# S5 preparation in fewer, wider VectorE operations, and twelve of the first block's 24 gate tiles emitted from inside it

## The chip, the cores and the metric

One core of one Trainium2 chip runs the whole kernel. The metric is the device time of one execution in microseconds. Everything is fp32; matrix products against large weights are done as three fp32r products of split operands.

## The reference, cut to what matters

One layer of a streaming encoder is applied to 2048 + 16 prompt tokens and 64 sample tokens (2128 tokens of 1024 channels): a layer norm, one input projection, three recurrent branches (RWKV-7, S5, mLSTM), a gated sum of the branches, an output projection and a last layer norm.

```python
proj = (x @ p['w_in']).astype(F32)
rw_cols, rw_gate, s5_u, s5_gate, ml_qk, ml_v, ml_if, ml_o, ml_z, merge = split_cols(proj, IN_SIZES)
y_rw, ... = rwkv7_branch(rw_cols, rw_gate, ...)
y_s5, ... = s5_branch(s5_u, s5_gate, ...)
y_ml, ... = mlstm_branch(ml_qk, ml_v, ...)
gates = jax.nn.sigmoid(merge + p['b_merge']).reshape(x.shape[:2] + (N_BRANCH, D_MODEL))
merged = gates[..., 0, :] * (y_rw @ w_br_rw) + gates[..., 1, :] * (y_s5 @ w_br_s5) + gates[..., 2, :] * (y_ml @ w_br_ml)
# S5: lam_bar = exp(lam * dt); b_bar = ((lam_bar - 1) / lam) * b_mat
# hs = scan of lam_bar * h + b_bar @ u; y = real(c_mat @ hs) + d * u
```

The change touches two pieces: how the constant matrices of S5 are worked out on the chip (complex powers of `lam_bar`, times `b_bar` and `c_mat`), and when the `merge` columns of the projection are computed (24 tiles of 128 columns, the gate tiles).

## The kernel before, in words

The tokens are cut into five blocks; block 0 has 400 tokens, the next three 448, the last 384. In each block three generators run mixed by weights (`mix`): `rw_block` (six head pairs, each with a long chain of small operations), `ml_block`, and `s5_stream`. Each asks for projections: `proj` loads a 128-column tile of `w_in` and runs 24 matmuls on it (line 434, into PSUM tile `d`). In block 0 the tile comes raw from DRAM (line 404, two halves of 256 KB), ScalarE casts each half to `whi` (line 405), GpSimd subtracts to get `wlo` (line 406), and both go back to DRAM (line 411); later blocks load the split halves directly (line 425). Block 0 has 63 projections and 24 gate tiles, the same for the later blocks.

A gate tile is the same thing with its own buffers (`ghi`, `glo`, two halves each, so one tile deep; PSUM tile `f`, one buffer), then a tanh (line 1509) and a store. `gate_pass(b)` emits the 24 tiles after all generators of the block have ended. The activations `xh`, `xl` have one buffer each, so that the next block's copies land only when the last matmul of this block, a gate tile's, has read them. The raw weight buffers (three of them) are handed out in the order of emission, which is why no gate tile can start before the block's projections have been loaded.

`s5_setup` runs once, in block 0, as part of `s5_stream`: scalar work on 128x16 tiles, a table of powers per four state groups (`tab`, lines 1199 to 1212), the powers `pw`, the transposed C matrices, and a loop over 16 values of `q` (line 1259) that builds, per q, a scaled B (`bb`), `BL` (128x2x128), `CL` (128x2x144), two transposes (line 1274) and four K matmuls (line 1281). Its complex products go through `cmul`, six VectorE operations for each. All VectorE work of it is recorded at the helper's line 1132.

A scheduler orders each engine's instructions from the order of emission and from its own costs, so a change in emission reorders rows that the diff does not show. Loads, weight stores and the small transfers of the RWKV chain all stand in one queue, on SyncE.

Of the kernel before, what the change touches and what calls it, by code (L numbers as in the profile page):

```python
# [13 lines left out]
ALU = mybir.AluOpType  # L14
# [69 lines left out]
def tile_trunk(ctx: ExitStack, tc: tile.TileContext, I, O, dbg=None, parts=("rw", "s5", "ml", "mg")):  # L84
    nc = tc.nc
    V, S, G, PE = nc.vector, nc.scalar, nc.gpsimd, nc.tensor
    QQ = nc.sync
    blocks = make_blocks()
# [25 lines left out]
    def psum(shape, tag):  # L114
        return pt(ps, shape, tag, bufs=PSB[tag])
# [28 lines left out]
    TS = 8 * (NCM + 1)  # L144
# [970 lines left out]
    s5wo_d = pt(dram, (16, 128, 4, 128), "s5wo")  # L1115
# [6 lines left out]

    def s5_setup():
        A = [sA() for _ in range(4)]
        B = [sB() for _ in range(3)]
        nsm = [0]

        def sm():
            nsm[0] += 16
            return cut(A[1], nsm[0] - 16, (128, 16))  # L1130
# [46 lines left out]
        TT(pw[:, 0, 1], cs, zr, ALU.mult)  # L1177
        TT(pw[:, 1, 1], sn, zr, ALU.mult)

        def cmul(orr, oi, xr, xi, yr, yi, t):  # L1180
            TT(t, xi, yi, ALU.mult)
            TT(orr, xr, yr, ALU.mult)
            TT(orr, orr, t, ALU.subtract)
            TT(t, xi, yr, ALU.mult)
            TT(oi, xr, yi, ALU.mult)
            TT(oi, oi, t, ALU.add)

        for _ in range(3):
            double()
# [9 lines left out]
        for i in range(4):  # L1199
            tab = cut(flat("tab", TS), 0, (128, 4, 2, NCM + 1))  # L1200
            V.memset(tab[:, :, 0, 0:1], 1.0)
            V.memset(tab[:, :, 1, 0:1], 0.0)
            V.tensor_copy(tab[:, :, 0, 1], cs[:, 4 * i:4 * i + 4])
            V.tensor_copy(tab[:, :, 1, 1], sn[:, 4 * i:4 * i + 4])
            m = 1
            while m < NCM:
                n = min(m, NCM - m)
                o = slice(m + 1, m + 1 + n)
                y = [tab[:, :, ri, m:m + 1].to_broadcast((128, 4, n)) for ri in range(2)]
                cmul(tab[:, :, 0, o], tab[:, :, 1, o], tab[:, :, 0, 1:n + 1], tab[:, :, 1, 1:n + 1], y[0], y[1],  # L1210
                     cut(A[0], 288, (128, 4, 32))[:, :, :n])
                m *= 2
            nc.scalar.dma_start(s5t_d[i], tab.rearrange("p q r n -> p (q r n)"))
        yield
        ta = cut(A[0], 288, (128, 8, 16))
        for m in (1, 2, 4):
            b1 = lambda x: x[:, m:m + 1].to_broadcast((128, m, 16))
            cmul(pw[:, 0, m + 1:2 * m + 1], pw[:, 1, m + 1:2 * m + 1], pw[:, 0, 1:m + 1], pw[:, 1, 1:m + 1],
                 b1(pw[:, 0]), b1(pw[:, 1]), ta[:, :m])
# [3 lines left out]
        fr, fi, den, lm = sm(), sm(), sm(), sm()  # L1223
        TT(den, ar, ar, ALU.mult)
        TT(lm, ai, ai, ALU.mult)
        TT(den, den, lm, ALU.add)
# [24 lines left out]
        kz = cut(flat("tab", TS), 0, (16, 15, 16))  # L1251
        G.memset(kz[:, 0:7, :], 0.0)
        bt = cut(A[1], 336, (128, 2, 16))
        bb = cut(A[1], 304, (128, 2, 16))
        tb = cut(B[0], 256, (128, 9, 16))
        BL = cut(B[1], 0, (128, 2, 8, 16))
        CL = cut(B[2], 0, (128, 2, 9, 16))
        for q in range(16):
            for ri, nm in enumerate(("s5_b_re", "s5_b_im")):
                nc.sync.dma_start(bt[:, ri], I[nm][0, 2 * q:2 * q + 2].rearrange("a p h -> (a p) h"))  # L1260
            e = lambda x: x[:, q:q + 1].to_broadcast((128, 16))
            cmul(bb[:, 0], bb[:, 1], bt[:, 0], bt[:, 1], e(fr), e(fi), tb[:, 0])
            pe = lambda ri, n: pw[:, ri, 0:n, q:q + 1].to_broadcast((128, n, 16))
            pr = lambda ri: pwr[:, ri, :, q:q + 1].to_broadcast((128, 8, 16))
            be = lambda ri: bb[:, ri:ri + 1, :].to_broadcast((128, 8, 16))
            ce = lambda ri: cT[ri][:, q:q + 1, :].to_broadcast((128, 9, 16))
# [3 lines left out]
            wB = cut(w5(), 0, (128, 2, 128))  # L1270
            for ri in range(2):
                nc.scalar.dma_start(s5wo_d[q, :, 2 + ri, :], CL[:, ri, 1:9, :].rearrange("p j h -> p (j h)"))
                p = psum((128, 128), "o")
                PE.transpose(p, BL[:, ri].rearrange("p s h -> p (s h)"), ident)
                S.copy(wB[:, ri], p)
            nc.sync.dma_start(s5wi_d[q // 2, :, 2 * (q % 2):2 * (q % 2) + 2, :], wB)
            for g in range(2):
                r = slice(64 * g, 64 * g + 64)
                p = psum((16, 128), "o")
                for ri in range(2):  # L1280
                    PE.matmul(p, bb[r, ri, :], CL[r, ri, 0:8, :].rearrange("p j h -> p (j h)"),
                              start=ri == 0, stop=ri == 1)
                S.copy(kz[:, 7:15, :].rearrange("x j h -> x (j h)"), p)
                nc.scalar.dma_start(K_d[2 * q + g], kz)
            if q % 2:
                yield
        for g in range(2):
# [145 lines left out]
    def s5_stream(b):  # L1433
        for g in spend:
            yield from g
        d = yield from s5_proj(b)
        if b.first:
            yield from s5_setup()
            spend[:] = [s5_block(b, *d)]
        else:  # L1440
            spend[:] = []
            yield from s5_block(b, *d)

    def drain(g):
        for _ in g:
            pass
# [64 lines left out]

    def merge_pass():
        TBS = (768, 768, 576)
# [258 lines left out]
```

## Time and profile before

| | us |
|---|---|
| median of 3 runs (lowest to highest) | 4073.04 (4065.59 to 4080.69) |
| the profiled execution, its time | 4056.56 |
| its span, first to last instruction | 4054.6 |
| TensorE busy, share of the span | 3753.2, 93% |
| VectorE busy, share of the span | 2508.7, 62% |
| mean granted TensorE clock | 0.965 |

The windows below are cut where a new RWKV head pair starts (its first matmul at line 532): 186, 308, 424, 544 and 654 us in block 0, and 865 and 965 us for the first two head pairs of block 1. In `f` and `d` of the rows, `f` is a gate tile's PSUM tile and `d` a projection's.

### The profile page before, as it was taken

What the parts mean: (1) busy time and instruction counts of PE and PEld (TensorE: products, weight loads), DVE (VectorE), ACT (ScalarE), POOL (GpSimd) and SP (SyncE); (2) the same over time, 40 slices, a digit from 0 to 9 for tenths busy, and PEclk for the clock granted to TensorE, in tenths of its full rate; (3) what the DMA queues carried; (4) which work ended last, traced back from release to release, by engine and by line L of the source; (5) the groups of instructions that cost most, each with busy time, mean ns of one, the idle gap of its engine ahead of it and who ended that gap; (6) DMA issues with size and microseconds to landing.
All of it is one profiled execution on the core that took longest, in us unless ns stands there. A gap on an engine that the chain in (4) does not pass through costs nothing. (4 is left out here: it accounts for less than half of the span.)

```text
span 4054.6 us, 76802 instructions
## 1 busy us (share of the span) xinstructions
PE 3753.2 (93%) x27032; PEld 3319.8 (82%) x27032; DVE 2508.7 (62%) x8247; ACT 1204.0 (30%) x2626; POOL 669.3 (17%) x947
## 2 busy tenths in 40 slices
PE   6987778989999999999999999999999998999997
PEld 5876567878888878888878888878988887999997
DVE  7668885546556656656674665664675555457476
ACT  5433232323222222222232232223232232222222
POOL 5433132300000000000000000100000000233335
PEclk9988798999999999999999999999999998999999
DMA  8986378876657686666666565767677666566565
GB/s 255 290 250 198 89 223 238 273 246 189 202 185 225 193 254 188 194 195 203 204 214 219 170 212 183 219 203 225 219 228 229 202 200 172 159 195 206 153 188 161
DMA packets 820735, 836.67 MB, mean 206 GB/s; under 512 B 226118, under 2 KB 580654, under 8 KB 820350
## 3 DMA queue, kind: packets, MB, share of 16 engines
q1 hardware_dynamic: 737790, 759.00, 60.6%
q10 hardware_dynamic: 82560, 72.76, 6.0%
q8 instruction: 214, 3.51, 0.4%
q14 instruction: 171, 1.40, 0.1%
HBM read 635.40 MB, written 198.18 MB: 206 GB/s over the span
## 5 line engine op out<-in xcount | busy, mean ns | idle before, releaser
L434 PE MATMUL d<-xh,whi 128*128 128x448 f32 (+2 forms) x2520 | 940.3, 373 | 33.2 <-ACT whi L405 6.9
L434 PE MATMUL d<-xh,wlo 128*128 128x448 f32 (+2 forms) x2520 | 926.1, 368 | 5.8 <-POOL wlo L406 4.1
L434 PE MATMUL d<-xl,whi 128*128 128x448 f32 (+2 forms) x2520 | 924.6, 367 | 0.0
L434 PEld LDWEIGHTS d<-xh,whi 128*128 128x128 f32 x2520 | 481.5, 191 | 83.4 <-issue 17.4
L434 PEld LDWEIGHTS d<-xh,wlo 128*128 128x128 f32 x2520 | 480.9, 191 | 44.9 <-POOL wlo L406 8.1
L434 PEld LDWEIGHTS d<-xl,whi 128*128 128x128 f32 x2520 | 481.6, 191 | 34.0 <-issue 8.2
L406 POOL TENSOR_TENSOR wlo<-wraw,whi 128x512 fp32r<-128x512 f32 (+1 forms) x310 | 404.1, 1312 | 605.3 <-ACT whi L405 538.9
L434 PE MATMUL f<-xh,ghi 128*128 128x448 f32 (+2 forms) x912 | 348.1, 382 | 39.9 <-DMA ghi<-wsp 29.4
L434 PE MATMUL f<-xh,glo 128*128 128x448 f32 (+2 forms) x912 | 342.0, 375 | 3.0 <-DMA glo<-wsp 2.6
L434 PE MATMUL f<-xl,ghi 128*128 128x448 f32 (+2 forms) x912 | 337.9, 371 | 0.0
L405 ACT CAST whi<-wraw 128x512 fp32r<-128x512 f32 (+1 forms) x310 | 179.8, 586 | 421.5 <-PE z L1565 79.2
L618 DVE TENSOR_TENSOR Ztmp<-Uin,Z 128x60 f32<-128x60 f32 (+24 forms) x930 | 205.1, 221 | 117.8 <-DMA Uin<-Ud 105.2
L434 PEld LDWEIGHTS f<-xh,ghi 128*128 128x128 f32 x912 | 177.9, 195 | 60.5 <-DMA ghi<-wsp 21.7
L620 DVE TENSOR_TENSOR Z<-Z,Ztmp 128x60 f32<-128x60 f32 (+24 forms) x930 | 210.0, 226 | 13.0
L1565 PE MATMUL z<-ya,whi 128*128 128x384 f32 (+1 forms) x832 | 196.5, 321 | 0.0
L434 PEld LDWEIGHTS f<-xh,glo 128*128 128x128 f32 x912 | 177.4, 194 | 20.7 <-DMA glo<-wsp 6.4
L434 PEld LDWEIGHTS f<-xl,ghi 128*128 128x128 f32 x912 | 178.2, 195 | 10.5 <-issue 1.3
L946 DVE SCALAR_TENSOR_TENSOR X<-X,PT 128x448 f32<-128x448 f32 (+2 forms) x180 | 127.1, 706 | 42.9 <-ACT X L944 39.6
L1565 PEld LDWEIGHTS z<-ya,whi 128*128 128x128 f32 x832 | 144.4, 188 | 0.0
L1565 PE MATMUL z<-ya,wlo 128*128 128x384 f32 (+1 forms) x416 | 133.8, 322 | 0.0
L1565 PE MATMUL z<-yb,whi 128*128 128x384 f32 (+1 forms) x512 | 120.1, 320 | 2.1 <-DVE lq2i L251 1.8
L701 DVE COPY XV<-tr 64x512 f32<-64x512 f32 (+2 forms) x60 | 36.5, 614 | 134.9 <-ACT XV L700 134.2
(738 smaller groups left out, 6815.8 us busy)
## 6 DMA issues: line engine op xcount, KB each, us to landing
whi<-wsp SPq DMA_DIRECT2D x504, 256.0 KB
wlo<-wsp SPq DMA_DIRECT2D x504, 256.0 KB
ghi<-wsp SPq DMA_DIRECT2D x192, 256.0 KB
glo<-wsp SPq DMA_DIRECT2D x192, 256.0 KB
wraw<-in_w_in_dram SPq DMA_DIRECT2D x174, 256.0 KB
wsp<-whi SPq DMA_DIRECT2D x126, 256.0 KB
wsp<-wlo SPq DMA_DIRECT2D x126, 256.0 KB
w<-s5wo SPq DMA_DIRECT2D x80, 256.0 KB
```

The lines of the kernel that those rows point to most:

```text
L405: S.copy(h[:, :n, :M], raw[:, :n, :M])
L406: G.tensor_tensor(l[:, :n, :M], raw[:, :n, :M], h.bitcast(F32)[:, :n, :M], ALU.subtract)
L434: PE.matmul(p, a[k], c, start=i == 0, stop=i == 3 * KD - 1)
L618: V.tensor_tensor(t3, Uin[:, j:j + 1, j + 1:32].to_broadcast((128, m, n)), Z[:, 0:m, j:j + 1].to_broadcast((128, m, n)), ALU.mult)
L620: V.tensor_tensor(Z[:, 0:m, j + 1:32], Z[:, 0:m, j + 1:32], t3, ALU.add)
L701: V.tensor_copy(PX[hs[1], c0:c0 + n, 0:3:2, :], p[hs[1], :n])
L946: V.scalar_tensor_tensor(acc[:, :w], raw[:, j:j + w], pcol("conv_w", 12 * j + ti), acc[:, :w], ALU.mult, ALU.add)
L1565: PE.matmul(p, a[k], c[:, sl], start=i == 0, stop=i == n - 1)
```

## The change

Three things. First, `cmul` works on real and imaginary part together: two products of double width and two sums instead of four products and two sums, so four operations for six; the sign of `CL`'s imaginary part is folded into its last one, and `bb` is made for eight q at once (two loads of 8 q each, per part, where there were 32 small ones). Second, the two K products of a q share one PSUM tile and the two transposes share another; the K rows have two SBUF buffers; a q has one store of `CL` instead of two. Third, the gate tiles of block 0 become a generator, `gate1`, and `s5_stream` takes one tile from it each time `s5_setup` yields. It yields twelve times: eleven tiles stand between its steps and the twelfth behind its last; `gate_pass` drains the other twelve.

```diff
-        B = [sB() for _ in range(3)]
+        B = [sB() for _ in range(4)]
...
-        def cmul(orr, oi, xr, xi, yr, yi, t):
-            TT(t, xi, yi, ALU.mult)
-            TT(orr, xr, yr, ALU.mult)
-            TT(orr, orr, t, ALU.subtract)
-            TT(t, xi, yr, ALU.mult)
-            TT(oi, xr, yi, ALU.mult)
-            TT(oi, oi, t, ALU.add)
+        def cmul(out, x, yr, yi, u):
+
+            TT(out(None), x, yr, ALU.mult)
+            TT(u(None), x, yi, ALU.mult)
+            TT(out(0), out(0), u(1), ALU.subtract)
+            TT(out(1), out(1), u(0), ALU.add)
...
         for q in range(16):
-            for ri, nm in enumerate(("s5_b_re", "s5_b_im")):
-                nc.sync.dma_start(bt[:, ri], I[nm][0, 2 * q:2 * q + 2].rearrange("a p h -> (a p) h"))
-            e = lambda x: x[:, q:q + 1].to_broadcast((128, 16))
-            cmul(bb[:, 0], bb[:, 1], bt[:, 0], bt[:, 1], e(fr), e(fi), tb[:, 0])
...
-            cmul(BL[:, 0], BL[:, 1], be(0), be(1), pr(0), pr(1), tb[:, 0:8])
-            cmul(CL[:, 0], CL[:, 1], ce(0), ce(1), pe(0, 9), pe(1, 9), tb)
-            V.tensor_scalar(CL[:, 1], CL[:, 1], -1.0, None, ALU.mult)
+            if q % 8 == 0:
+                for ri, nm in enumerate(("s5_b_re", "s5_b_im")):
+                    nc.sync.dma_start(bb[:, ri], I[nm][0, 2 * q:2 * q + 16].rearrange("(q a) p h -> (a p) q h", a=2))
+                e = lambda x: x[:, None, q:q + 8, None].to_broadcast((128, 2, 8, 16))
+                TT(u8, bb, e(fi), ALU.mult)
+                TT(bb, bb, e(fr), ALU.mult)
+                TT(bb[:, 0], bb[:, 0], u8[:, 1], ALU.subtract)
+                TT(bb[:, 1], bb[:, 1], u8[:, 0], ALU.add)
...
+            cmul(at(BL, 1), pr, be(0), be(1), at(u8, 1))
...
+            TT(CL, pe, ce(0), ALU.mult)
+            TT(u9, pe, ce(1), ALU.mult)
+            TT(CL[:, 0], CL[:, 0], u9[:, 1], ALU.subtract)
+            V.scalar_tensor_tensor(CL[:, 1], CL[:, 1], -1.0, u9[:, 0], ALU.mult, ALU.subtract)
...
         if b.first:
-            yield from s5_setup()
+            for _ in s5_setup():
+                next(gate1)
+                yield
...
-    def gate_pass(b):
+    def gates(b):
         T = b.T
         for j in range(24):
...
             nc.sync.dma_start(g_d[b.i][128 * j:128 * j + 128, :], t[:, :T])
+            yield
+
+    gate1 = gates(blocks[0])
+
+    def gate_pass(b):
+        drain(gate1 if b.first else gates(b))
```

On VectorE, one q of the loop before (`sA` and `sB` are the scratch tiles that hold `bb`, `pw`, `BL`, `CL`):

```order
L1132 TENSOR_TENSOR sB_3107<-sA_3104 128x16
L1132 TENSOR_TENSOR sB_3108<-sA_3104,sB_3107 128x128 x2
L1132 TENSOR_TENSOR sA_3104<-sA_3104,sB_3107 128x16
L1132 TENSOR_TENSOR sB_3107<-sA_3104,sB_3107 128x128
L1132 TENSOR_TENSOR sB_3108<-sB_3108,sB_3107 128x128
...
L1132 TENSOR_TENSOR sB_3107<-sA_3106,sA_3103 128x144
L1132 TENSOR_TENSOR sB_3109<-sB_3109,sB_3107 128x144
...
L1269 TENSOR_SCALAR sB_3109<-sB_3109 128x144
```

And one q of the loop now:

```order
L1132 TENSOR_TENSOR sA_3104<-sB_3107,sB_3110 128x256
L254 TENSOR_TENSOR mqa_4698<-mrs_4696 128x2
L1132 TENSOR_TENSOR sB_3108<-sB_3108,sA_3104 128x128 x2
L255 SCALAR_TENSOR_TENSOR mqa_4698<-mqa_4698,mve_4694 128x2
L1132 TENSOR_TENSOR sA_3104<-sA_3103,sA_3106 128x288
...
L1132 TENSOR_TENSOR sB_3109<-sA_3103,sA_3105 128x288
L717 TENSOR_TENSOR Hw_4858<-tr_4859,Wc_3540 128x448
L1132 TENSOR_TENSOR sB_3109<-sB_3109,sA_3104 128x144
L1283 SCALAR_TENSOR_TENSOR sB_3109<-sB_3109,sA_3104 128x144
```

A q had 19 operations and has 8, with four more for every eight q; the elements that they pass over are nearly the same.

On GpSimd, the stretch that follows the third head pair's copy of `Wc` (line 554), before:

```order
L406 TENSOR_TENSOR wlo_5291<-wraw_5292,whi_5290 128x512
L406 TENSOR_TENSOR wlo_5485<-wraw_5486,whi_5484 128x512
L406 TENSOR_TENSOR wlo_5493<-wraw_5494,whi_5492 128x512
L198 TENSOR_TENSOR X_3673<-X_3673 128x2x64 x4
L449 MEMSET rv_5115 128x48
L406 TENSOR_TENSOR wlo_5866<-wraw_5867,whi_5865 128x512
```

And now:

```order
L406 TENSOR_TENSOR glo_4608<-wraw_4609,ghi_4607 128x512
L406 TENSOR_TENSOR glo_4616<-wraw_4617,ghi_4615 128x512
L406 TENSOR_TENSOR wlo_5049<-wraw_5050,whi_5048 128x512
L406 TENSOR_TENSOR glo_5004<-wraw_5005,ghi_5003 128x512
L406 TENSOR_TENSOR glo_5012<-wraw_5013,ghi_5011 128x512
L406 TENSOR_TENSOR wlo_5057<-wraw_5058,whi_5056 128x512
L406 TENSOR_TENSOR wlo_5186<-wraw_5187,whi_5185 128x512
```

Subtracts of gate tiles (`glo`) now stand between those of projections (`wlo`).

On GpSimd again, the end of block 0, from the last gate tiles to the first `Wc` of block 1; before, 40 subtracts for gate tiles stand between the last `Wc` of block 0 and this one:

```order
L406 TENSOR_TENSOR glo_8596<-wraw_8597,ghi_8595 128x512
L406 TENSOR_TENSOR glo_8604<-wraw_8605,ghi_8603 128x512
L554 COPY Wc_9200<-W_9135 128x7
```

And now, where the stretch holds 11 of them:

```order
L554 COPY Wc_7176<-W_7093 128x7
L741 MEMSET Ss_7117 128x64
L406 TENSOR_TENSOR glo_8067<-wraw_8068,ghi_8066 128x512
...
L756 COPY Scar_405<-Hw_7065 128x64
L406 TENSOR_TENSOR glo_8239<-wraw_8240,ghi_8238 128x512
...
L406 TENSOR_TENSOR glo_8292<-wraw_8293,ghi_8291 128x512
L610 MEMSET Z_9335 128x256
...
L554 COPY Wc_8888<-W_8823 128x7
```

Five and a half gate tiles are left for the stretch between two blocks where there were twenty.

## Rows read from the trace of the kernel before

**Rows 1.** Two of the page's 40-slice lines, in tenths.
```profile
PE   6987778989999999999999999999999998999997
...
PEclk9988798999999999999999999999999998999999
```

**Rows 2.** Windows by head pair: length, busy us (instructions) per engine, clock, DMA.
```profile
core 0: us, PE busy (x) PEld busy (x) DVE busy (x) ACT busy (x) POOL busy (x), PEclk, DMA share, GB/s
186.00:308.00 122.00, 105.23 (x735) 95.57 (x734) 77.25 (x236) 45.35 (x99) 51.50 (x55) 0.92 0.86 250
308.00:424.00 116.00, 84.01 (x599) 73.21 (x598) 104.43 (x503) 38.11 (x92) 36.09 (x45) 0.84 0.59 182
424.00:544.00 120.00, 91.30 (x626) 69.17 (x626) 99.81 (x400) 41.93 (x119) 25.50 (x45) 0.79 0.46 140
544.00:654.00 110.00, 85.63 (x620) 72.77 (x619) 76.10 (x269) 36.92 (x94) 30.22 (x41) 0.86 0.74 220
654.00:865.00 211.00, 186.98 (x1446) 168.22 (x1444) 115.66 (x417) 63.75 (x140) 59.66 (x54) 0.94 0.88 266
865.00:965.00 100.00, 88.48 (x681) 75.65 (x681) 58.95 (x200) 30.38 (x69) 5.44 (x15) 0.95 0.59 184
```

**Rows 3.** Windows of line 434 alone (projections and gate tiles): PE, PEld, clock, DMA.
```profile
186.00:308.00 122.00, 79.79 (x375) 70.94 (x373) 0.92 0.86 250
308.00:424.00 116.00, 47.03 (x218) 41.88 (x218) 0.84 0.59 182
424.00:544.00 120.00, 41.48 (x187) 36.57 (x188) 0.79 0.46 140
544.00:654.00 110.00, 54.91 (x245) 47.14 (x245) 0.86 0.74 220
654.00:865.00 211.00, 134.75 (x630) 117.57 (x630) 0.94 0.88 266
```

**Rows 4.** PE timeline: start, duration, instruction; two matmuls of one tile.
```profile
343.01 0.35 PE L434 MATMUL d<-xl,whi 128*128 128x400 f32 x1
343.19 0.34 PE L434 MATMUL d<-xh,wlo 128*128 128x400 f32 x1
```

**Rows 5.** Line 434 from 654 to 830 us: durations, first and last start.
```profile
L434 PE MATMUL d<-xh,whi x1: 720/720/720, 829.6 to 829.6; 128*128 128x448 f32 x1
```

**Rows 6.** Line 1509, the gate tiles' tanh, from 654 to 830 us.
```profile
L1509 ACT ACTIVATE gt<-f,hbm x22: 572/589/594, 654.3 to 825.3; 128x400 f32<-128x400 f32 x22
```

**Rows 7.** Waits from 654 to 830 us: total us, times, longest.
```profile
POOL glo L406 <- ACT ghi L405: 73.7, 29, 6.9
ACT ghi L405 <- PE f L434: 49.9, 21, 5.9
```

**Rows 8.** Timeline of VectorE and GpSimd: start, duration, instruction.
```profile
309.77 3.42 POOL L406 TENSOR_TENSOR wlo<-wraw,whi 128x512 fp32r<-128x512 f32 x2
310.77 1.19 DVE L457 SCALAR_TENSOR_TENSOR rv<-PT,rv 128x1 f32<-128x1 f32 x1
...
353.56 0.16 DVE L1132 TENSOR_TENSOR sA<-tab 128x16 f32<-128x16 f32 x1
353.65 0.17 DVE L1132 TENSOR_TENSOR tab<-tab 128x32 f32<-128x32 f32 x1
...
425.71 0.30 DVE L1132 TENSOR_TENSOR sB<-sA,sA 128x144 f32<-128x144 f32 x1
425.93 0.29 DVE L1132 TENSOR_TENSOR sB<-sB,sB 128x128 f32<-128x128 f32 x1
...
616.38 0.20 DVE L620 TENSOR_TENSOR Z<-Z,Ztmp 128x35 f32<-128x35 f32 x1
...
616.82 1.26 POOL L406 TENSOR_TENSOR glo<-wraw,ghi 128x512 fp32r<-128x512 f32 x1 [2.10 <-PE o L1281]
616.83 1.29 DVE L620 TENSOR_TENSOR Z<-Z,Ztmp 128x28 f32<-128x28 f32 x1
```

**Rows 9.** Window of line 406 alone, GpSimd busy (instructions), clock, DMA.
```profile
308.00:654.00 346.00, 70.56 (x53) 0.83 0.59 179
```

**Rows 10.** What SyncE's queue waited for, 308 to 654 us: total us, times, longest.
```profile
SPq L411 <- ACT whi L405: 19.0, 11, 4.4
```

More of the change, by code (lines that the diff above doesn't have):

```diff
@@ L1178, in s5_setup, with at, f @@
         TT(pw[:, 1, 1], sn, zr, ALU.mult)
-        def cmul(orr, oi, xr, xi, yr, yi, t):
-            TT(t, xi, yi, ALU.mult)
-            TT(orr, xr, yr, ALU.mult)
-            TT(orr, orr, t, ALU.subtract)
-            TT(t, xi, yr, ALU.mult)
-            TT(oi, xr, yi, ALU.mult)
-            TT(oi, oi, t, ALU.add)
+        def cmul(out, x, yr, yi, u):
[3 more added lines that the diff above has]
+            TT(out(1), out(1), u(0), ALU.add)
+        def at(t, axis):
+            def f(ri):
+                if ri is None:
+                    return t
+                return t[:, ri] if axis == 1 else t[:, :, ri]
+            return f
         for _ in range(3):
@@ L1208, in s5_setup @@
                 o = slice(m + 1, m + 1 + n)
-                y = [tab[:, :, ri, m:m + 1].to_broadcast((128, 4, n)) for ri in range(2)]
-                cmul(tab[:, :, 0, o], tab[:, :, 1, o], tab[:, :, 0, 1:n + 1], tab[:, :, 1, 1:n + 1], y[0], y[1],
-                     cut(A[0], 288, (128, 4, 32))[:, :, :n])
+                y = [tab[:, :, ri:ri + 1, m:m + 1].to_broadcast((128, 4, 2, n)) for ri in range(2)]
+                cmul(at(tab[:, :, :, o], 2), tab[:, :, :, 1:n + 1], y[0], y[1],
+                     at(cut(B[i % 2], 0, (128, 4, 2, 32))[:, :, :, :n], 2))
                 m *= 2
@@ L1214, in s5_setup @@
         yield
-        ta = cut(A[0], 288, (128, 8, 16))
+        ta = cut(B[1], 0, (128, 2, 8, 16))
         for m in (1, 2, 4):
-            b1 = lambda x: x[:, m:m + 1].to_broadcast((128, m, 16))
-            cmul(pw[:, 0, m + 1:2 * m + 1], pw[:, 1, m + 1:2 * m + 1], pw[:, 0, 1:m + 1], pw[:, 1, 1:m + 1],
-                 b1(pw[:, 0]), b1(pw[:, 1]), ta[:, :m])
+            y = [pw[:, ri:ri + 1, m:m + 1].to_broadcast((128, 2, m, 16)) for ri in range(2)]
+            cmul(at(pw[:, :, m + 1:2 * m + 1], 1), pw[:, :, 1:m + 1], y[0], y[1], at(ta[:, :, :m], 1))
         pwr = cut(B[0], 0, (128, 2, 8, 16))
@@ L1222, in s5_setup @@
             V.tensor_copy(pwr[:, :, j], pw[:, :, 7 - j])
-        fr, fi, den, lm = sm(), sm(), sm(), sm()
+        fr, fi, den, lm = dt, zi, k, w2
         TT(den, ar, ar, ALU.mult)
@@ L1250, in s5_setup @@
         yield
[L1251 to L1255, printed above, removed]
+        kt = flat("tab", TS)
+        kz = [kt[64 * g:64 * g + 16, 0:240].rearrange("p (j h) -> p j h", h=16) for g in range(2)]
+        for g in range(2):
+            G.memset(kz[g][:, 0:7, :], 0.0)
+        bb = cut(B[3], 0, (128, 2, 8, 16))
+        u9 = cut(A[1], 168, (128, 2, 9, 16))
+        u8 = cut(A[1], 168, (128, 2, 8, 16))
         BL = cut(B[1], 0, (128, 2, 8, 16))
@@ new lines, in s5_setup @@
+            r8_ = q % 8
+            be = lambda ri: bb[:, ri, None, r8_:r8_ + 1, :].to_broadcast((128, 2, 8, 16))
+            pr = pwr[:, :, :, q:q + 1].to_broadcast((128, 2, 8, 16))
+            cmul(at(BL, 1), pr, be(0), be(1), at(u8, 1))
+            ce = lambda ri: cT[ri][:, None, q:q + 1, :].to_broadcast((128, 2, 9, 16))
+            pe = pw[:, :, 0:9, q:q + 1].to_broadcast((128, 2, 9, 16))
+            TT(CL, pe, ce(0), ALU.mult)
+            TT(u9, pe, ce(1), ALU.mult)
+            TT(CL[:, 0], CL[:, 0], u9[:, 1], ALU.subtract)
@@ L1270, in s5_setup @@
+            V.scalar_tensor_tensor(CL[:, 1], CL[:, 1], -1.0, u9[:, 0], ALU.mult, ALU.subtract)
             wB = cut(w5(), 0, (128, 2, 128))
+            nc.scalar.dma_start(s5wo_d[q, :, 2:4, :], CL[:, :, 1:9, :].rearrange("p r j h -> p r (j h)"))
+            p = psum((128, 2, 128), "o")
             for ri in range(2):
-                nc.scalar.dma_start(s5wo_d[q, :, 2 + ri, :], CL[:, ri, 1:9, :].rearrange("p j h -> p (j h)"))
-                p = psum((128, 128), "o")
-                PE.transpose(p, BL[:, ri].rearrange("p s h -> p (s h)"), ident)
@@ L1275, in s5_setup @@
-                S.copy(wB[:, ri], p)
+                PE.transpose(p[:, ri], BL[:, ri].rearrange("p s h -> p (s h)"), ident)
+            S.copy(wB, p)
             nc.sync.dma_start(s5wi_d[q // 2, :, 2 * (q % 2):2 * (q % 2) + 2, :], wB)
-            for g in range(2):
[L1278 to L1284, printed above, removed]
+            p = psum((128, 128), "o")
@@ L1285, in s5_setup @@
+            for ri in range(2):
+                for g in range(2):
+                    r = slice(64 * g, 64 * g + 64)
+                    PE.matmul(p[64 * g:64 * g + 16], bb[r, ri, r8_, :], CL[r, ri, 0:8, :].rearrange("p j h -> p (j h)"),
+                              start=ri == 0, stop=ri == 1)
+            for g in range(2):
+                S.copy(kz[g][:, 7:15, :].rearrange("x j h -> x (j h)"), p[64 * g:64 * g + 16])
+                nc.scalar.dma_start(K_d[2 * q + g], kz[g])
             if q % 2:
```

4 lines of the change are left out of this document (removed).

## The prediction, made before the changed kernel ran

> **What bounds the kernel now.** I read the page first: TensorE's busy line and its clock line are full, except in the first fifth, where the busy line falls to 7 and 8 tenths and the clock line to 7 to 9 [rows 1]. So the loss lies in block 0, and I cut it by head pairs [rows 2]. From 186 to 308 us TensorE is busy 86% and the DMA engines 86%. From 308 to 654 us, three head pairs, TensorE is busy 261 of 346 us at clocks of 0.79 to 0.86, the DMA engines 46 to 74%, while VectorE is busy 104 of 116, 100 of 120 and 76 of 110 us, 280 in all. This is the stretch in which S5's preparation runs, and VectorE is the fullest engine of its first two head pairs. TensorE gets little there: line 434 has 218, 187 and 245 matmuls, at 24 to a tile 9.1, 7.8 and 10.2 tiles, against 375, or 15.6, in the head pair before [rows 3].
>
> Then 654 to 865 us, twice as long as any other head pair. From 654 to 825 us 22 gate tiles finish, 171 us over 21 steps, 8.1 us each [rows 6], while a tile's 24 matmuls need 24 x 0.183 = 4.4 us [rows 4]. The waits say why: the subtract waits for the cast, and the cast for the matmuls of the tile before, which hold the single-tile buffers [rows 7]. No projection runs in all that time. The first one of block 1 starts at 829.6 us, right behind the last gate tile [rows 5], since the activations' only buffers are read until then. So the gate tiles' chain sets when block 1 begins. From 865 us on the kernel is bound by TensorE (88% here, nines behind), and what block 0 gains comes through to the end.
>
> **The change, part by part.** The sum is made for the profiled execution, 4056.6 us, span 4054.6; the median of the runs shown is 16.5 us above it, and I carry that over. Where rows move, I counted them in the changed order between the same marks.
>
> *VectorE's own work.* The tables lose 48 operations (4 x 6 x 2), the powers 6, the q loop 304 - 136 = 168: 222 in all. The elements stay, but for the sign pass, 16 x 144. What an operation costs is the step from one start to the next, since they overlap: 0.09 us for 16 elements (duration 0.16), 0.22 for 144 (duration 0.30) [rows 8]. That is some 0.07 us fixed and 1 ns an element. So 222 x 0.07 + 2304 x 0.001 = 18 us go, not the 35 that durations would give. The cover of these 18 is discussed below.
>
> *GpSimd in VectorE's way.* Gate tiles bring their subtracts with them. By the order 81 subtracts stand in the three head pairs, where the trace has 53 [rows 9]; 28 more. Where a subtract runs, a VectorE operation beside it is stretched: 0.20 us becomes 1.29 [rows 8]. Along the timeline from 308 to 654 us this happens at 41 of 52 subtracts that start there, the first at 309.8 and the last at 616.8 us, both shown, by some 1.05 us each. 28 x 0.8 x 1.05 = 24 us come back. Bounds: 0, if they fall where VectorE waits, and 28 x 1.1 = 31.
>
> The Trainium skill ("SBUF — State Buffer", Who interferes with whom) has the rule: VectorE operations with two SBUF inputs and GpSimd operations that read SBUF share a port pair that one holds for its whole instruction. Read strictly, every one of the 28 would cost its 1.26 us, 35 us instead of 24, and the sum below would be 11 us worse. The trace agrees with the rule where VectorE is busy; about a fifth of the subtracts here met no such operation.
>
> *Work that shifts with it.* By the order the three head pairs hold 1034 VectorE instructions where there were 1170, though S5's fall by 217: 81 others move in from the head pairs beside. At 280 / 1172 = 0.24 us a piece [rows 2] that is 19 us. VectorE's sum for 308 to 654 us: 280 - 18 + 24 + 19 = 305 us. At the share of the whole stretch (280 of 346, 81%) it needs 377 us, at that of its fullest head pair (104 of 116, 90%) 339. I take the middle, 358: 12 us more than now, bounds -7 and +31.
>
> Does the rest fit into 358 us? 25.4 projections and 16.4 gate tiles by the order, 41.8 x 4.4 = 184 us, and the other TensorE work that is there now, 261 - 143 = 118 us [rows 2, 3], make 302, or 84%: as 186 to 308 us, so yes, at the edge. DMA: 16.4 x 1.5 MB on top of 62 MB, 87 MB, 243 GB/s against 250 in that same head pair. ScalarE's and GpSimd's parts of a gate tile (some 1.8 and 2.6 us) lie on engines that are busy a third of the time.
>
> *The gap between the blocks.* Behind the last head pair of block 0 five and a half gate tiles are left by the order, where there were twenty. If the chain alone counts, 14.5 x 8.1 = 118 us go. But this stretch also has S5's block and tails of the other branches, 187 - 135 = 52 us of TensorE beside line 434 (630 matmuls there now). By the order it will hold 6.6 gate tiles of block 0, 2 of block 1 and 7 projections of block 1, 29 + 10 + 34 us (4.4 us x 448 / 400 = 4.9 us a tile of 448 columns), and three quarters of the small rows, 39 us: 112 us, at the share of now (187 of 211, 89%) 126. By the rate of 186 to 308 us, with more small rows, 136. I take 126: 85 us less, bounds -118 and -75. What is late next is TensorE itself.
>
> *Behind it.* 865 to 965 us gets 1.2 tiles fewer and 66 small rows more, -6 + 8 = +2 us. At its end the projections stand as they did, but 2.6 gate tiles more are done: 2.6 x 4.9 = 12 us that later head pairs need not spend.
>
> *Small edits at nothing.* Fewer B loads, one `CL` store for two, one PSUM tile for two, a second buffer for K: they shorten waits on SyncE and ScalarE that the VectorE row covers. If that cover were gone they could only help, by a few us; the fourth `sB` buffer is used by no one else until the preparation ends, 0. The load of eight q at once puts one wait of some us in VectorE's row, twice.
>
> Sum: +12 - 85 + 2 - 12 = -83 us. 4073 - 83 = 3990 us.
>
> **The rivals.** *(a) The tiles fill for nothing.* TensorE has 85 idle us from 308 to 654, and 41 and 54% of the DMA engines' time is free in its first two head pairs. If the stretch keeps its length or loses 7, and the gap loses the whole 118: -7 - 118 + 2 - 12 = -135, 3938 us. For it: the idle time. Against it: VectorE at 90%, and 24 us coming in.
>
> *(b) VectorE pays more.* Every moved subtract stretches an operation by its whole 1.26 us [rows 8], 35 us for 24, all of VectorE's sum is needed at the lower share, and the gap keeps its upper end: +31 + 11 - 75 + 2, with 5 us of surplus instead of 12, is -36, 4037 us. For it: by the order the head pair from 308 us holds 35 subtracts for 19, and 60% more elements of S5's work. Against it: 11 of 52 subtracts stretched nothing. This is what the rule of the shared port, above, would make of it.
>
> *(c) The gap is not the gate tiles'.* If block 1 waits for something else that ends at 830 us (its activations from DRAM, S5's block), the gate tiles leave and nothing moves: 12 us of stretch against the surplus, 4073 us. Against it: the 4 us between the last gate tile's tanh and the first projection [rows 5, 6].
>
> *(d) Slower: the queue.* Each gate tile puts four stores, two loads and one more store into SyncE's queue, where the RWKV chain's transfers stand. A store there waits for its cast, now 19.0 us for 11, 1.7 each and 4.4 at most [rows 10]. If all four stores of each of the twelve tiles hold up the chain, 12 x 4 x 1.7 = 83 us, the gain is eaten; at 2.4 us each, 115 us, the time is 32 above now, 4105. The point is 1.7 us a store, and all on the chain. Against it: from 186 to 308 us the queue carries 15.6 tiles a head pair and the head pair takes 122 us, hardly more than the others.
>
> **How the numbers follow.** My forecast, a gain between 50 and 120 us, gets 0.57; its own range is 3953 to 4023. (a) gets 0.15, (b) 0.15, (c) 0.07, (d) 0.06. A measurement of this kernel tells about 0.5%, 20 us, from no change. Faster by more than that: the forecast, (a), and nearly all of (b), 0.87. Within: (c), 0.07. Slower: (d), 0.06. The range reaches over (a) and (b), 3938 to 4045, and leaves out (c), (d) and the far end of (a).
>
> **What would show it.** Right: from 308 to about 665 us TensorE busy over 80% at a clock near 0.95, some 16 gate tiles in it, VectorE over 85% busy; the first projection of block 1 at about 730 to 750 us instead of 829.6; block 1's later head pairs about 100 us each as now. The VectorE step is right if S5's operations cost about 18 us less without the stretched ones, and the subtract step if there are some 60 stretched ones before the last gate tile of block 0's last head pair. Wrong would be a first projection of block 1 later than 800 us, or head pairs of 140 us and more from 308 us on with SyncE's stores as what the RWKV chain waits for.

## The result, and the profile after

| | us |
|---|---|
| before, median of 4 runs (lowest to highest) | 4074.3 (4065.6 to 4080.7) |
| after, median of 4 runs | 4021.9 (4013.8 to 4031.9) |
| ratio, 95% interval | 0.9888 (0.9871 to 0.9905) |
| forecast, range | 3990, 3938 to 4045 |

Faster by 52 us; 83 had been forecast. The direction held and the time lies inside the range, though at the slow end of the forecast's own part of it (3953 to 4023); the size is 0.63 of the forecast. The profiled execution after took 4013.8 us, its span is 4012.0.

In the page's slices, what answers to [rows 1] is this: the dip in TensorE's first fifth is shallower (one slice of eight at seven tenths where there were three), and of the clock's first eight slices only the third and the fifth stand below nine tenths, at eight.

```profile
PE   6988788999999899999999999999989998999997
PEclk9989899999999999999999999999999998999999
```

The windows, cut at the same head pairs as [rows 2] (columns as there):

```profile
185.00:302.00 117.00, 102.14 (x711) 91.52 (x709) 70.19 (x216) 43.46 (x95) 48.96 (x54) 0.91 0.86 248
302.00:437.00 135.00, 120.64 (x845) 106.23 (x840) 119.32 (x486) 52.79 (x123) 55.35 (x60) 0.96 0.84 261
437.00:559.00 122.00, 98.28 (x746) 81.08 (x745) 106.67 (x327) 49.92 (x132) 38.34 (x56) 0.90 0.68 206
559.00:668.00 109.00, 95.54 (x710) 84.86 (x709) 78.42 (x229) 41.18 (x88) 40.28 (x45) 0.92 0.89 268
668.00:796.00 128.00, 119.79 (x984) 107.03 (x982) 73.94 (x284) 35.30 (x80) 20.90 (x27) 0.95 0.83 254
796.00:897.00 101.00, 93.35 (x785) 79.65 (x785) 68.54 (x265) 33.06 (x80) 6.05 (x14) 0.95 0.64 194
```

The three head pairs of the preparation take 366 us where they took 346, and VectorE is busy 304 us in them (forecast 358 and 305). The stretch between the blocks takes 128 us where it took 211 (forecast 126). At the second head pair of block 1 the kernel is 68 us ahead, 897 against 965 us. The sum had -71 us there (+12 - 85 + 2); measured are +20 - 83 + 1, and 6 us that it did not have, gained ahead of these head pairs. At the end 43 us are left between the two profiled executions. So 25 us are lost in code that nobody edited.

To see where, I cut each execution at points of equal work: where TensorE has done 22, 62 and 86% of its matmul columns, each matmul counted as its columns and 48 more (in block 1, in block 3, at the start of the merge). The windows of before, of after, and of a second profiled execution of before (run e5, below):

```profile
0.00:1070.00 1070.00, 891.02 (x6260) 772.31 (x6261) 719.00 (x2553) 379.24 (x863) 309.28 (x430) 0.91 0.73 223
1070.00:2612.00 1542.00, 1494.90 (x11051) 1274.40 (x11051) 927.45 (x3247) 428.34 (x941) 91.92 (x225) 0.99 0.66 205
2612.00:3555.00 943.00, 894.31 (x6716) 806.75 (x6716) 544.20 (x1848) 269.58 (x615) 71.12 (x140) 0.98 0.66 204
```

```profile
0.00:990.00 990.00, 866.37 (x6231) 757.33 (x6233) 692.80 (x2313) 372.76 (x840) 309.86 (x426) 0.94 0.79 242
990.00:2544.00 1554.00, 1494.09 (x11079) 1272.90 (x11078) 938.99 (x3266) 434.90 (x951) 91.36 (x232) 0.99 0.65 203
2544.00:3511.00 967.00, 909.08 (x6724) 818.88 (x6723) 543.40 (x1845) 268.90 (x613) 71.16 (x139) 0.97 0.65 200
```

```profile
0.00:1073.00 1073.00, 889.47 (x6260) 768.58 (x6261) 721.58 (x2553) 378.59 (x863) 311.21 (x430) 0.91 0.73 222
1073.00:2628.00 1555.00, 1502.49 (x11051) 1280.42 (x11049) 929.79 (x3249) 429.58 (x944) 91.42 (x226) 0.98 0.66 203
2628.00:3571.00 943.00, 894.21 (x6719) 807.38 (x6718) 542.27 (x1845) 268.84 (x615) 71.31 (x140) 0.98 0.67 204
```

Up to 22% the gain is 80 to 83 us (12 more than by head pairs, which is what the sum had put down for gate tiles done ahead): 55 us less idle time of TensorE (1070 - 891 = 179, now 990 - 866 = 124), and 25 us less busy time for the same work, since the clock of that stretch rose from 0.91 to 0.94. Behind it, 1554 + 967 = 2521 us stand against 2485 and 2498: 23 to 36 us are lost again. Of the 36, 22 are idle time and 14 busy time. Against both executions of before 24 us are lost between 62 and 86%; between 22 and 62% it is 12 us against the first and nothing against the second.

A hole that opens at the end of block 1 (TensorE's timeline of after; start, duration, in brackets the idle time before and what ended it):

```profile
1391.20 0.72 PE L1348 MATMUL o<-sA,w 128*64 128x56 f32 x16
1398.61 3.63 PE L1391 MATMUL o<-sA,w 128*128 128x56 f32 x16 [6.70 <-DMA w<-s5wo]
1406.91 0.95 PE L662 MATMUL tr<-Z,AT 32*32 32x32 f32 x26 [4.67 <-DVE Z L656]
```

```profile
1379.00:1399.00 20.00, 9.19 (x60) 7.12 (x61) 6.05 (x20) 0.63 (x1) 0.00 (x0) 0.83 0.94 271
1399.00:1419.00 20.00, 12.99 (x175) 11.69 (x175) 3.51 (x7) 4.58 (x12) 0.73 (x5) 0.65 0.84 275
```

And the same place before:

```profile
1454.00:1474.00 20.00, 15.99 (x140) 12.66 (x140) 7.75 (x24) 1.12 (x4) 0.00 (x0) 0.66 0.68 213
1474.00:1494.00 20.00, 19.44 (x166) 14.74 (x165) 12.05 (x31) 11.85 (x29) 0.74 (x5) 1.00 0.65 203
```

S5's product waits 6.7 us for weights that arrive while the DMA engines are 94% busy, the gate tiles of the block are all done by 1390 us, and TensorE is busy 22 us of 40 at a clock of 0.65 to 0.83, against 35 of 40. No line there was edited.

But about half of what this hole costs had been won just ahead of it. From 22 to 32 and from 32 to 34% of the work, after and before:

```profile
990.00:1362.00 372.00, 364.15 (x2727) 314.92 (x2726) 239.49 (x835) 104.18 (x224) 28.46 (x62) 1.00 0.66 206
1362.00:1471.00 109.00, 88.64 (x652) 69.01 (x651) 43.00 (x122) 24.70 (x54) 0.73 (x5) 0.89 0.72 225
```

```profile
1070.00:1450.00 380.00, 367.80 (x2757) 317.02 (x2757) 235.33 (x843) 100.16 (x219) 25.80 (x57) 0.99 0.67 210
1450.00:1541.00 91.00, 85.78 (x607) 68.66 (x606) 42.49 (x115) 24.92 (x58) 0.74 (x5) 0.92 0.77 241
```

The two stretches together take 481 us after and 471 before (474 in the second execution). The larger loss, the 24 us between 62 and 86%, is 9 us of idle and 15 of busy time; no run here shows what it comes from.

### The profile page after: what moved, and what is told of

It reads as the page before. It is cut to its first block, busy times and chain, and to the rows that moved or that the text cites. A ratio compares the mean times of both kernels' runs of the same rounds, so it can differ in the third digit from the quotient of the medians.

```text
span 4012.0 us, 76369 instructions
## 1 busy us (share of the span) xinstructions
PE 3742.1 (93%) x27032; PEld 3316.3 (83%) x27032; DVE 2490.1 (62%) x8025; ACT 1202.5 (30%) x2610; POOL 668.4 (17%) x948
## 4 chain that ended last, share of the span: by engine, by line
PE 62%; DVE 15%; DMA 13%; issue 3%; SPq 2%; ACT 2%; POOL 1%; ACTq 0%; DVEq 0%; POOLq 0%
PE d L434 26%; PE f L434 9%; PE z L1588 7%; PE g L1588 3%; DMA xT<-X 2%; PE py L728 1%; DVE Ztmp L618 1%; DVE Z L620 1%; PE tr L581 1%; PE d L1435 1%; DMA E<-rd 1%; DMA Uin<-Ud 1%; PE tr L707 1%; PE tr L699 1%; DMA X<-in_x_prompt_dram 1%
## 5 line engine op out<-in xcount | busy, mean ns | idle before, releaser
L1526 ACT ACTIVATE gt<-f,hbm 128x448 f32<-128x448 f32 (+2 forms) x114 | 70.0, 614 | 178.5 <-PE f L434 140.5
```

## The experiments

All of them, by the same points of equal work (us; "behind" is from 22% to the end of the span):

| kernel | to 22% | behind | 22 to 62% | 62 to 86% | median | ratio to before (95%) |
|---|---|---|---|---|---|---|
| before, two executions | 1070, 1073 | 2984, 2999 | 1542, 1555 | 943, 943 | 4070 to 4074 | 1 |
| after | 990 | 3022 | 1554 | 967 | 4021.9 | 0.9888 (0.9871 to 0.9905) |
| e1 tiles alone | 1037 | 3041 | 1576 | 963 | 4079.1 | 1.0007 (0.9992 to 1.0022) |
| e2 wide alone | 1064 | 3011 | 1537 | 973 | 4070.5 | 0.9998 (0.9985 to 1.0012) |
| e3 two tiles a step | 975 | 3020 | 1560 | 959 | 4000.5 | 0.9827 (0.9812 to 0.9843) |
| e4 tile behind the step | 1015 | 3042 | 1568 | 970 | 4057.9 | 0.9970 (0.9958 to 0.9982) |
| e6 gate's low part zero | 1003 | 3039 | 1565 | 974 | 4043.4 | 0.9925 (0.9910 to 0.9940) |
| e7 S5 earlier in block 1 | 1007 | 3034 | 1585 | 950 | 4042.3 | 0.9923 (0.9906 to 0.9939) |
| e8 two tiles, behind the step | 970 | 3047 | 1562 | 982 | 4019.3 | 0.9870 (0.9855 to 0.9884) |
| e9 before, steps shifted | 1054 | 3020 | 1565 | 951 | 4078.5 | 1.0008 (0.9994 to 1.0022) |
| e10 before, a step less | 1079 | 3028 | 1578 | 950 | 4111.0 | 1.0087 (1.0062 to 1.0112) |
| e11 narrow, two tiles a step | 994 | 3025 | 1577 | 947 | 4030.1 | 0.9901 (0.9869 to 0.9933) |

The rows below are the windows of the three head pairs of the preparation, as one window each. That of before and that of after:

```profile
308.00:654.00 346.00, 260.95 (x1842) 215.14 (x1842) 280.34 (x1170) 116.96 (x305) 91.82 (x131) 0.83 0.59 179
```

```profile
302.00:668.00 366.00, 314.46 (x2297) 272.17 (x2293) 304.42 (x1039) 143.89 (x342) 133.97 (x160) 0.93 0.80 244
```

**e1, the tiles alone.** Before, with `gate1` taken from in `s5_stream`:

```diff
-            yield from s5_setup()
+            for _ in s5_setup():
+                next(gate1)
+                yield
```

> The kernel before with the eleven gate tiles emitted between the steps of the preparation, and the preparation in its old, narrow operations (no wide ones). My theory: the moved gate tiles carry the gain by emptying the stretch between the blocks, and the wide operations are worth only the 18 us of VectorE that I put on them. Then the first projection of block 1 comes at 740 to 755 us (after: 729, before: 830), and the time is some 10 to 25 us above the changed kernel's 4022: 4030 to 4047. Rival 1 (the two parts need each other: without the wide operations VectorE is over-full and the tiles only lengthen the three head pairs): first projection of block 1 at 790 us or later, 4060 to 4075. Rival 2 (the gain beyond some 50 us is anyway given back behind block 0, by S5's chain at the end of block 1): first projection at 745, time equal to the changed kernel's within 8 us.

```profile
310.00:688.00 378.00, 315.92 (x2137) 269.95 (x2137) 304.83 (x1173) 135.25 (x341) 124.61 (x156) 0.86 0.73 223
```

A miss for my theory: the first projection of block 1 came at 775 us, between my theory's and rival 1's, and the time is that of before. To 22% it gains 33 to 36 us, and more than that, 42 to 57, is lost behind. In this stretch 14.2 gate tiles run where after has 16.4, and TensorE's clock is 0.86 against 0.93.

**e2, the wide operations alone.** After, with the tiles taken out:

```diff
-            for _ in s5_setup():
-                next(gate1)
-                yield
+            yield from s5_setup()
```

> The changed kernel with its wide operations, but all 24 gate tiles of block 0 behind the head pairs as before. My theory: VectorE loses 18 us of its 280 in the three head pairs, the gap of 211 us between the blocks stays, so the first projection of block 1 comes 10 to 18 us earlier than before, at 812 to 820 us, and the time is 4056 to 4070. Rival 1 (the wide operations carry the gain; the tiles are filling): first projection below 790 us, time below 4045. Rival 2 (the preparation doesn't bound the three head pairs): first projection at 826 to 832, time 4070 to 4078.

```profile
308.00:659.00 351.00, 267.70 (x1926) 229.42 (x1925) 259.98 (x972) 121.86 (x297) 100.79 (x135) 0.83 0.62 187
```

VectorE is busy 260 us where it was 280, as the sum had it, and the stretch is 5 us longer, not shorter. First projection at 819 us, as I expected; the time between my theory and rival 2. So VectorE's sum doesn't set these three head pairs.

**e3, two tiles a step.** One line more in after: `next(gate1, None)` behind `next(gate1)`.

> The changed kernel with two gate tiles at each of the eleven steps, 22 of block 0's 24. My theory: the three head pairs of the preparation grow by some 11 x (4.4 to 5) = 50 us, since TensorE is then full in them, and the gap shrinks by as much, so the first projection of block 1 stands at 720 to 740 us, and the time is that of the changed kernel within 12 us. Rival 1 (each tile behind the head pairs costs its 8.1 us of chain, and each in them nothing): first projection at 660 to 690, time 3975 to 3990. Rival 2 (GpSimd's subtracts stretch VectorE's operations and there is no room): first projection at 760 or later, time 4040 or more.

```profile
311.00:679.00 368.00, 322.42 (x2340) 285.83 (x2334) 283.30 (x962) 149.41 (x345) 147.80 (x171) 0.95 0.86 266
```

A miss: with 22 gate tiles for 16.4 the stretch grows by 2 us, not 50. There was room: the clock rose to 0.95, and the DMA engines carry 266 GB/s. The first projection of block 1 comes at 682 us, as rival 1 had it; the time lies between rival 1's and my theory's. It is the fastest kernel of all, 21 us below after.

**e4, each tile behind the other streams' step.**

```diff
-                next(gate1)
                 yield
+                next(gate1)
```

> The changed kernel with each gate tile emitted just behind the other streams' step, not ahead of it: the same work, the same eleven tiles, in a slightly different order. It measures how much of the time is the order that happens to come out. Theory 1 (what was given back behind block 0 is a mechanism, S5's chain at the end of block 1, which holds the projections' buffers): the end of block 1 gives back 12 to 22 us here too, and the time is 4022 within 8. Theory 2 (it is the order that comes out anew with every edit): block 0 gains the same 80 to 90 us, the boundaries behind it come out otherwise, and the time differs from 4022 by 10 us or more either way.

The time is as theory 2 had it, but not its block 0, which gains 55 to 58 us to the 22% mark and not 80 to 90. In the medians the same work costs 36 us more; in the profiled executions it is 44, 25 by the 22% mark (14.0 gate tiles for 16.4 in the three head pairs) and 20 behind it.

**e5, before once more.**

> The kernel before once more, for a second profiled execution. The first one took 4056.6 us, 13 below the median of the 21 runs beside the experiments so far (4069.8). Between the third last projection phase and the merge (62 to 86% of TensorE's work) it is 16 to 29 us shorter than all five other kernels, the changed one among them. Theory 1 (that stretch of the profiled execution was a lucky one): a second execution takes 4065 to 4080, and 10 to 20 us of the difference to the first lie between 62 and 86%. Theory 2 (any edit makes the order in the last blocks worse): the second execution has that stretch within 5 us of the first.

My suspicion was wrong. The second execution has 62 to 86% of the work in 943 us, as the first; the 18 us between them lie mostly in 22 to 62%. So the first was a quick one, but not there, and what the others lose between 62 and 86% is real.

**e6, the gate tiles without GpSimd's reads.** Block 0's gate tiles get zeros for the weights' low part:

```diff
-            G.tensor_tensor(l[:, :n, :M], raw[:, :n, :M], h.bitcast(F32)[:, :n, :M], ALU.subtract)
+            if tag == "g":
+                G.memset(l.bitcast(F32)[:, :n, :M], 0.0)
+            else:
+                G.tensor_tensor(l[:, :n, :M], raw[:, :n, :M], h.bitcast(F32)[:, :n, :M], ALU.subtract)
```

> The changed kernel, in which block 0's gate weights are multiplied without their low part: GpSimd writes zeros to the low tile instead of subtracting the cast from the raw weight, so none of its operations of a gate tile reads SBUF; the matmuls, stores and loads stay. My theory by the sum (VectorE's busy time sets the three head pairs): of 31 gate subtracts there, the stretches of some 25 go, 25 us of VectorE's 304, and the three head pairs lose 15 to 25 of their 366 us; the first projection of block 1 comes at 704 to 715 instead of 729. Rival 1 (VectorE isn't what sets them; the wide-only kernel lost 20 us of VectorE there and no time): VectorE's sum falls by 15 to 25, the three head pairs keep their length within 6 us. Rival 2 (zeros written by GpSimd hold VectorE as much as the subtract did): VectorE's sum within 6 us of 304.

```profile
309.00:669.00 360.00, 308.01 (x2231) 271.51 (x2231) 259.19 (x960) 141.95 (x336) 108.52 (x161) 0.92 0.80 246
```

Rival 1, and more of it: VectorE's sum falls by 45 us, partly because 79 operations fewer stand in the window, and the three head pairs lose 6. The first projection of block 1 comes at 728 us, as after. And though GpSimd has less to do, the time is over 20 us above after's. Of the 32 zero writes (0.53 us each) some 25 lie beside VectorE operations, and 3 or 4 of them beside one over 0.3 us longer than others of its form that met no other work of GpSimd; of the 50 subtracts that are left, some 30 hold an operation for 0.7 us and more. The Trainium skill ("SBUF — State Buffer", Who interferes with whom) says that a VectorE operation with two SBUF inputs contends with GpSimd's reads and not with its mere writes; the trace agrees but for those 3 or 4, and what lengthened these is not shown.

**e7, S5 earlier in block 1.** `MIXES[1]` from `0.8,1.3,2` to `0.8,1.3,1.5`.

> The changed kernel with the S5 stream of block 1 taken more often in the mix (weight 1.5 for 2), so that its last products are emitted sooner. The changed kernel loses 18 us against the one before at the end of block 1, where TensorE is busy 22 of 40 us at a clock of 0.65 to 0.83, S5's products wait for their weights (6.7 us), and no projection or gate tile is left to fill the time. Theory 1 (S5's part came last there): with S5 earlier the stretch from 32 to 34% of TensorE's work falls from 108 to 88 to 95 us, and the time to 4002 to 4012. Theory 2 (the order of any part comes out anew): the 32 to 34% stretch changes either way, other stretches of blocks 0 and 1 change by 5 us and more too, and the time is anywhere within 4005 to 4060.

Theory 2. The stretch that it was meant for went from 108 to 79 us, and from 22 to 32% of the work 34 us were lost that after doesn't lose. The hole at the end of block 1 is not one cause that can be taken away by itself.

**e8, two tiles a step, behind it.** The edit of e4 on e3.

> Two gate tiles at each step, each pair emitted just behind the other streams' step and not ahead of it: to the kernel with two tiles a step (4000 us) what the yield-first kernel (4058) was to the changed one (4022). Theory 1 (the place of the tiles in the order matters: behind the step they come one head pair later, and fewer fall into it): the three head pairs hold 2 gate tiles fewer than the 22, and it takes 10 to 25 us more than 4000. Theory 2 (with enough tiles to fill TensorE's pauses the place doesn't matter): within 8 us of 4000. Theory 3 (a lottery): any time within 3990 to 4045, and the difference lies in blocks that the edit doesn't touch.

The time alone would fit theories 1 and 3; its parts fit theory 3 alone: 22.9 gate tiles in the three head pairs, 5 us ahead of e3 at 22%, and 27 us lost behind.

**e9 and e10, controls on before.** Neither moves any work by intent:

```diff
-            if q % 2:
+            if q % 2 == 0:
                 yield
```

```diff
         K_d = pt(dram, (32, 16, 15, 16), "Kd")
-        yield
```

> The kernel before, with the steps of the preparation's q loop ending after the even q and not the odd: the same instructions, none moved by intent, a control. All eight kernels tried so far, with edits in block 0 alone, lose 19 to 55 us against the kernel before behind 22% of TensorE's work, where no line was edited. Theory 1 (the order there comes out anew with every edit, and the one that the kernel before has is a favourable one among many): block 0 within 10 us of before, behind it 15 to 50 us lost, 4080 to 4120. Theory 2 (what is lost behind block 0 comes from the gate tiles or the wide operations): the time stays at 4060 to 4080.

> The kernel before with one pause of the preparation taken away (two of its steps made one): a second control, the same instructions again. Theory 1 (an order of its own, less favourable than that of before): 15 to 50 us lost behind 22% of TensorE's work, 4080 to 4120 in all. Theory 2: 4060 to 4080. If the two controls differ by more than 15 us from each other, what is lost is a matter of the order that comes out, not of one cause.

The windows from 22 to 62 and from 62 to 86%, of e9:

```profile
1054.00:2619.00 1565.00, 1515.48 (x11029) 1283.27 (x11029) 927.24 (x3237) 429.64 (x943) 87.74 (x227) 0.98 0.66 202
2619.00:3570.00 951.00, 909.87 (x6740) 819.31 (x6737) 550.42 (x1856) 268.62 (x616) 75.61 (x141) 0.97 0.66 202
```

and of e10:

```profile
1079.00:2657.00 1578.00, 1513.18 (x10983) 1286.91 (x10984) 924.09 (x3228) 428.47 (x941) 87.65 (x225) 0.98 0.65 201
2657.00:3607.00 950.00, 900.48 (x6784) 811.22 (x6784) 547.95 (x1864) 269.69 (x618) 78.63 (x143) 0.98 0.67 202
```

Both lose there without a moved gate tile or a wide operation: 2516 and 2528 us against 2485 and 2498 of before; after has 2521. But they lose it mostly between 22 and 62%, and only 7 or 8 us between 62 and 86%, where after loses 24. e10's time is as theory 1 had it. e9's is that of before, as theory 2 had it, since its block 0 came out 16 to 19 us shorter, which neither theory had. The two controls differ by 32 us from each other, with the same instructions in another order.

**e11, narrow operations and two tiles a step.** The edits of e1 and e3 on before.

> The kernel before, narrow operations, with two gate tiles at each step. It closes the square: narrow and wide, 11 and 22 tiles. Up to 22% of TensorE's work the gains so far are 7 us (wide alone), 34 (narrow, 11 tiles), 80 (both) and 96 (wide, 22 tiles). Theory 1 (more gate tiles fill TensorE's pauses whatever VectorE does; the wide operations add some 20 us): gain at 22% of 65 to 80 us, the time 4020 to 4050. Theory 2 (with the narrow operations VectorE is the bound of the three head pairs, and more tiles only lengthen them): gain at 22% of 20 to 40 us, the time 4055 to 4090.

```profile
312.00:673.00 361.00, 317.69 (x2193) 269.42 (x2192) 311.93 (x1165) 139.21 (x345) 134.59 (x161) 0.94 0.79 242
```

Theory 1 on both counts. VectorE is as full as in any of them, 312 us of 361, and the tiles fit all the same.

## Why the prediction was right, and where its size was off

*The loss of block 0 and its place.* Right. The stretch was the one that [rows 2] showed, and the gap between the blocks went from 211 to 128 us. The first projection of block 1 starts at 729.0 us, just ahead of the 730 to 750 forecast, and 3 us behind the start of the last gate tile's tanh; before it was 829.6 [rows 5]. Its row, and that of the tanh (first and last start):

```profile
729.05 0.47 PE L434 MATMUL d<-xh,whi 128*128 128x448 f32 x1 [0.72 <-DMA xh<-xT]
```

```profile
L1526 ACT ACTIVATE gt<-f,hbm x7: 572/588/593, 678.1 to 726.0; 128x400 f32<-128x400 f32 x7
```

Of the gate tiles' own chain, 15.5 us of waits are left behind 668 us (window 668 to 729), where [rows 7] had 73.7:

```profile
POOL glo L406 <- ACT ghi L405: 15.5, 9, 4.4
ACT ghi L405 <- PE f L434: 6.0, 3, 3.0
```

*VectorE's own work.* The 18 us held. Over the whole span VectorE is busy 2477.3 us with the wide operations alone, against 2508.7 and 2510.9 before, and 2490.1 after against 2515.2 with the tiles alone: 25 to 34 us. But these sums hold the operations that GpSimd stretched as well. With each operation beside a GpSimd one counted at no more than the median length of its form elsewhere, the six executions with narrow operations (before twice, e1, e9, e10, e11) come to 2324 to 2331 us and the seven with wide ones to 2304 to 2313: 19 us less in the mean. So the step from start to start gave the right size, as the prediction's own sign asked (without the stretched ones); the rest is fewer stretched operations.

*GpSimd in VectorE's way.* The 81 subtracts stand there as counted, 50 and 31 in GpSimd's groups from 302 to 668 us, against [rows 9]:

```profile
L406 POOL TENSOR_TENSOR wlo<-wraw,whi 128x512 fp32r<-128x512 f32 x50 | 68.6, 1376 | 77.5 <-ACT whi L405 71.1 <-PE o L1295 4.2 <-DMA xT<-X 0.9
L406 POOL TENSOR_TENSOR glo<-wraw,ghi 128x512 fp32r<-128x512 f32 x31 | 40.9, 1325 | 52.1 <-ACT ghi L405 36.6 <-ACT gt L1526 3.9 <-DMA wraw<-in_w_in_dram 3.2
```

Some 55 of the 81 hold a VectorE operation for 0.7 us and more; by the same count it was some 40 of 52 before. So some 16 came in, not 22: some 17 us at 1.05, not 24. What the stretches make of VectorE's busy time in these head pairs, counted as in the paragraph before, rose from 42 to 60 us, which says the same. Rival (b), in which every one counts, is out: by it VectorE's sum would have been 316 us.

*The three head pairs.* The sum of 305 us was met (304), and 366 us lies in the bounds around 358. TensorE is busy 86% there at 0.93 and 16.4 gate tiles run, as I had it; VectorE with 83% is under the 85 that I had named. But the step from the one to the other is not borne out. VectorE's sum was 259, 260, 283, 304, 305 and 312 us in e6, e2, e3, after, e1 and e11, and the length 360, 351, 368, 366, 378 and 361. They don't go together. What does set the length of these head pairs I have not shown. The order alone moves it: in the controls e9 and e10, with the instructions of before, the same three take 335 and 355 us with VectorE busy 278 and 279 us:

```profile
305.00:640.00 335.00, 259.38 (x1835) 213.12 (x1834) 277.52 (x1169) 116.70 (x304) 91.59 (x132) 0.83 0.61 185
308.00:663.00 355.00, 272.80 (x1878) 225.15 (x1877) 279.21 (x1171) 120.04 (x309) 95.06 (x133) 0.80 0.59 178
```

These two differ by 20 us, as much as the 366 us of after and the 346 of before. What the runs show is that TensorE has room there, as rival (a) said: 22 gate tiles run in 368 us and 16.4 in 366.

*The clock.* I had it only in the share of busy time. The mean clock mixes the full and the half level, so in after a clock of 0.93 for 0.83 in that stretch means that the time at the lower level, 1.2 GHz, fell from 2 x 0.17 x 346 = 118 to 2 x 0.07 x 366 = 51 us. That is about half of why the parts are worth more together. To 22%, the wide operations gain 6 to 9 us alone, 11 tiles with narrow operations 33 to 36, both 80 to 83. The windows to 22% of e1 (tiles alone) and of e2 (wide alone):

```profile
0.00:1037.00 1037.00, 891.50 (x6260) 773.72 (x6261) 720.41 (x2543) 372.53 (x856) 306.88 (x425) 0.92 0.76 230
0.00:1064.00 1064.00, 888.63 (x6266) 774.39 (x6267) 690.81 (x2332) 377.99 (x845) 310.62 (x430) 0.91 0.74 224
```

Alone, neither shortens TensorE's busy time by more than 2.4 us; together they take 25 us off it. Of the 41 us that both give beyond the two alone (80 - 33 - 6), 23 are busy time and 18 idle time. The Trainium skill ("TensorE: Matmul & The Clock Gate", HAM oscillation) has the rule that TensorE's clock falls when waits leave it idle; the rows agree: 85 us idle and a clock of 0.83 in the three head pairs before, 52 us and 0.93 after, 46 us and 0.95 in e3.

*Rivals (a), (c) and (d).* (a) had the room right and the rest wrong: the head pairs grew by 20 us, and the gap lost 83 us, not 118. (c) and (d) are out. The gap was the gate tiles'. SyncE's waits for casts did grow: at line 411, from 19.0 us for 11 [rows 10] to these from 302 to 668 us,

```profile
SPq L411 <- ACT whi L405: 27.9, 16, 4.7
SPq L411 <- ACT ghi L405: 10.7, 9, 2.6
```

and the length of the head pairs doesn't follow them: in e3 they come to 29 us where after has 39, and the head pairs are 2 us longer.

```profile
SPq L411 <- ACT whi L405: 20.5, 17, 4.1
SPq L411 <- ACT ghi L405: 8.9, 7, 3.4
```

*The step that failed:* "what block 0 gains comes through to the end". To 22% the sum held: 83 forecast, 80 to 83 measured. Behind it 23 to 36 us went in the profiled executions, some 30 in the medians (82 - 52). No part of the change is needed for such a loss. Each of the eleven edited kernels (ten of them edited in block 0 alone), the two controls among them, needs 3011 to 3047 us behind the 22% mark, and before 2984 and 2999. The code there is the same, but the scheduler orders it anew: between 36 and 60% of the work, the share of VectorE's instructions that a comparison of the two sequences finds in the same order as before is 0.25 in after, 0.24 in e9 and 0.22 in e10 (over 0.99 in the second execution of before). So the order that the kernel before had is favourable, an edit of block 0 draws another, and the draws cost 12 to 63 us. These are single executions, and two of before differ by 15 us in this part, so the smallest (e2) says little; the controls lose 21 to 44. Neither half of the change decides it: between 62 and 86%, where after loses 24 us, e2 without the tiles loses 30, e1 without the wide operations 20, and e11 with twice the tiles 4. That the loss of after itself is the order's and nothing else's is argued from these kernels, not shown by itself. What makes the old order favourable I can't name: I showed one hole that another order opens, at the end of block 1, and e7 closed it at the price of a loss just ahead of it.

So it is in part luck that the time fell inside the range: e4, the same work in another order, took 4057.9 us, outside of it.

## What to carry to other kernels

Where a scheduler orders the code, an edit is two things: what it does in its place, and a new order of all that follows. Read the first at points of equal work, before and behind the edit, and measure the second by edits that change nothing; here it is worth 12 to 63 us in single executions, as much as the change. And a pause of the matrix engine that also lowers its clock can take more filler than the full engine beside it suggests: two gate tiles a step (4000.5 us) beat one (4021.9), and to the 22% mark two are ahead in all three pairs of kernels that differ in this alone, by 15 us (e3 and after), 45 (e8 and e4) and 43 (e11 and e1).

## What the hardware showed that was not expected

The same kernel's two profiled executions lie 18 us apart (4054.6 and 4072.6), 13 us of it between 22 and 62% of the work and none between 62 and 86%. GpSimd's zero writes went with a lengthened VectorE operation in 3 or 4 of 32 cases, its subtracts in some 30 of 50. Of two kernels with the same instructions (e9 and e10), one takes 32 us longer in the medians. And of the gain up to the 22% mark, 25 of 80 us came from TensorE doing the same matmuls in less busy time.
